# Attention in a hybrid decoder layer: softmax denominators from a column of ones beside each head's value rows

## The chip, the cores and the metric

The kernel runs on one core of a Trainium2 chip. The metric is device time in microseconds for one execution of the whole layer. Five engines work side by side, each through its own instructions in order: TensorE (PE in the profile, its weight loads are PEld), VectorE (DVE), ScalarE (ACT), GpSimd (POOL) and SyncE (SP), which here issues transfers. Matrix products land in PSUM, eight banks of 128 x 512 float32; all else lies in SBUF.

## The reference, cut to what matters

One decoder layer on 512 tokens of width 1024, in float32: a SwiGLU feed-forward half step, a mixer, and a second half step. The mixer's input product gives channels for a gated recurrence (RG-LRU), its gate, and q, k, v for an attention with 8 heads of 64 and 2 key heads. Attention works in blocks of 128 queries against the block before and the block itself, and each head has a sink, a logit without a value:

```
scores = jnp.einsum("bnqkgd,bnjkd->bnkgqj", qb, k_band).astype(jnp.float32) * scale
...
scores = jnp.where(mask[None, :, None, None], scores, MASK_VALUE)
sink = sinks.astype(jnp.float32).reshape(1, 1, N_KV_HEADS, GQA_GROUP, 1, 1)
m = jnp.maximum(jnp.max(scores, axis=-1, keepdims=True), sink)
p = jnp.exp(scores - m)
denom = jnp.sum(p, axis=-1, keepdims=True) + jnp.exp(sink - m)
p = (p / denom).astype(v.dtype)
out = jnp.einsum("bnkgqj,bnjkd->bnqkgd", p, v_band)
...
y = jnp.concatenate([rms_norm(y_lru, g_lru_out), rms_norm(y_attn, g_attn_out)], axis=-1)
return y @ w_o
```

The window is 128, so a query sees exactly 128 keys: those up to itself in its own block, and the later part of the block before.

## The kernel before, in words

Each engine executes its instructions in the order in which the program names them; the order of all engines is written out by hand. Tiles come from pools: tiles with one tag share a fixed number of buffers, and a new tile takes a buffer as it is first written. If all are in use, that first write waits for the last reader of the tile that held the buffer. Three tags matter here. `bank` is the eight PSUM banks. `w` (helper `wt`) has eight buffers of 128 x 512. `t2k` has 38 buffers of 128 x 512 (`NT2K`), shared by the whole layer.

The first feed-forward (up to about 310 us) and the second (from about 530 us) are long series of matrix products. Between them stands the mixer. Weights are split into a rounded part and a remainder (`W.fill` and `W.take`: ScalarE rounds, VectorE subtracts), so that three products of the fast float32 form make one of full precision (`mm3`).

`masks` (line 1319) prepares, on GpSimd, a tile `home` of 128 x 2048: one quarter holds the mask value (`neg`), one the first block of q, one v, and its first 128 columns the first block of k. `in_parts` and the lines around 1510 to 1514 fill it; line 1514 copies v, four blocks of 128 tokens side by side, with both key heads' 64 columns in each.

Attention runs over eight units `(b, n)`: query block b, key head n, four heads each. A loop over `now` from 0 to 9 (line 1717) interleaves the units with other work; at each step the program names

1. `scores(now)`: for n = 0 the score products of the whole block b (four banks for b > 0, two for b = 0), then on VectorE the mask, the row maximum, `nm` (the negative maximum with the sink taken in) and `es` = nm + sink; and at some steps `W.fill`;
2. `pump`: two columns of `mm3` of the recurrence's gate product (`gt`), which fills TensorE's time;
3. `turn_p(now - 1)`: TensorE transposes the unit's four matrices of exponentials, ScalarE copies them to SBUF (`pa`), GpSimd cuts them into the current block's part (`pa`) and the previous block's (`pp`);
4. `exps(now)`: ScalarE, four exponentials of 128 x 128, each with an accumulated row sum (`dsum`), one exponential of `es`; GpSimd adds the two into `den`;
5. `run_due(now - 1)`: steps of the recurrence and of its gate (decay, tanh, scaling by R);
6. one more `pump`, and `values(now - 2)`: the products with v, four heads of 64 columns into half of a bank; both units of a block share the bank `po`. After the second unit VectorE inverts `den` and multiplies, 128 x 512, into `yn` (a `t2k` tile); ScalarE sums its squares later;
7. at now = 5 the four square roots of the recurrence on ScalarE with a table load on each side; at now = 6 their products and two scans on VectorE (`root_u`, `scan`); at now = 8 another scan and a weight split.

After the loop the four `yn` are scaled, transposed (line 1762, `atp`) and, with the recurrence's output, multiplied with `w_o`.

The `t2k` buffers in the middle of the loop: the mixer's input in 16 parts (`xh_mx`, `xl_mx`, read by the gate products until 456 us), `xc`, `r` and `th` with four tiles each, the parts of q for head pairs 0 to 2 (six tiles; those of pair 3 lie in another tag), the parts of k (two), and `up8`, the mask's bytes. `th` is first written at step ci + 1 for channel group ci, `G` at now = 6 and later. The parts of q and k are last read by the score products of block 3, at now = 6, head pair by head pair. In the program as laid out, the second `yn` takes the buffer of pair 0's q.

## Time and profile before

| | us |
|---|---|
| time, median of 3 runs | 845.54 (845.32 to 846.01) |
| span of the profiled execution | 843.6 |
| ScalarE busy, 434.40 to 438.00 and 438.00 to 442.00 | 3.57 of 3.60, 3.97 of 4.00 |
| VectorE busy, 424.00 to 434.40 | 10.02 of 10.40 |
| TensorE busy, 442.00 to 446.00 | 3.65 of 4.00 |
| accumulator reads of the exponentials | 24 and 8, 0.21 each |

The span is that of one profiled execution, from its first instruction to its last; the time of a run holds some 1.9 us more. A row of a timeline gives the start, the duration, the engine, the line of the program, the operation and its tiles; in brackets stands how long the engine had been idle and what released it. Starts lie closer than durations where an engine overlaps the end of one instruction with the start of the next. So the pitch, the distance between two starts, tells what an instruction costs its engine. In the chain of waits a row gives the start, the time that the chain spends there, the engine and the line.

### The profile page before, as it was taken

The page shows a single profiled execution, that of the slowest core. Times are in us where ns is not written, and L with a number is a line of the kernel's source. Part 1 is how long each engine was busy: PE and PEld are TensorE (multiplying, and loading weights), DVE is VectorE, ACT ScalarE, POOL GpSimd, SP SyncE. Part 2 cuts the span into 40 slices and gives each one's busy share as a digit, 9 for nine tenths or more (in the row PEclk, how much of TensorE's full clock was granted, in tenths as well). Part 3 has the DMA queues.
Part 4 walks back from the last instruction along what each step waited for, and adds up shares of the span by engine and source line. Part 5 has one row for each costly group of instructions (what it writes and reads, how often), then busy time and mean ns, then how long its engine had stood idle before and what let it go on. Part 6 is the DMA issues. An engine that isn't in the chain of part 4 may idle for free.

```text
span 843.6 us, 12618 instructions
## 1 busy us (share of the span) xinstructions
PE 834.5 (99%) x4568; PEld 722.6 (86%) x4568; DVE 732.7 (87%) x1020; ACT 523.8 (62%) x874; POOL 201.7 (24%) x214
## 2 busy tenths in 40 slices
PE   9999999999999999999999999999999999999996
PEld 8988888988988998997788899888888888888885
DVE  4978999998979865889899589799998998998996
ACT  6646856666666655456788457436757767666552
POOL 2023000140320333334646055112004113032001
PEclk9999999999999999999999999999999999999999
DMA  7249419397595799222511131169539939769742
GB/s 251 77 131 348 151 59 322 80 254 254 129 248 185 169 261 343 77 79 91 158 50 51 50 110 42 50 137 273 186 108 231 322 91 249 249 154 262 295 137 101
DMA packets 123615, 143.75 MB, mean 170 GB/s; under 512 B 23896, under 2 KB 81568, under 8 KB 123040
## 3 DMA queue, kind: packets, MB, share of 16 engines
q1 hardware_dynamic: 109232, 111.86, 41.6%
q0 software_dynamic: 14176, 30.94, 17.0%
q8 instruction: 36, 0.59, 0.3%
q14 instruction: 27, 0.22, 0.1%
q10 hardware_dynamic: 144, 0.13, 0.0%
HBM read 100.45 MB, written 40.89 MB: 168 GB/s over the span
## 4 chain that ended last, share of the span: by engine, by line
PE 97%; ACT 1%; DVE 1%; DMA 1%; issue 0%; POOL 0%; DVEq 0%; POOLq 0%; ACTq 0%
PE ab L955 10%; PE aa L955 10%; PE da L955 5%; PE db L955 5%; PE yaa L1345 3%; PE bb L955 3%; PE ba L955 3%; PE yda L1345 2%; PE ya L507 2%; PE ya L505 2%; PE ya L506 2%; PE a_first L1205 1%; PE aa L885 1%; PE yab L1875 1%; PE yab L1874 1%; PE yab L1876 1%
## 5 line engine op out<-in xcount | busy, mean ns | idle before, releaser
L1115 POOL DMA_DIRECT2D yp_a<-stage x42 | 36.9, 1085 | 181.2 <-ACT stage L1112 160.9
L1115 POOL DMA_DIRECT2D yp_b<-stage x42 | 36.4, 1091 | 144.6 <-ACT stage L1112 121.1
L505 PE MATMUL ya<-hha,whi_ad 128*128 128x512 f32 x62 | 24.1, 389 | 0.0
L506 PE MATMUL ya<-hla,whi_ad 128*128 128x512 f32 x62 | 24.1, 389 | 0.0
L507 PE MATMUL ya<-hha,wlo_ad 128*128 128x512 f32 x62 | 24.1, 389 | 0.0
L688 POOL TENSOR_TENSOR acca_r<-acca_r,sq_r 128x512 f32<-128x512 f32 x6 | 8.2, 1359 | 51.4 <-ACT sq_r L536 51.4
L1988 POOL TENSOR_TENSOR last<-yp,grow 128x512 f32<-128x512 f32 x3 | 3.9, 1290 | 57.7 <-DVE yp L1983 57.7
L524 PE MATMUL an<-xh_mx,whi_xl 128*128 128x256 f32 x64 | 15.8, 287 | 0.0
L1984 ACT ACTIVATE ysq<-yp 128x512 f32<-128x512 f32 (+1 forms) x9 | 5.3, 585 | 16.5 <-DVE yp L1983 16.0
L525 PE MATMUL an<-xh_mx,wlo_xl 128*128 128x256 f32 x64 | 15.5, 283 | 0.0
L505 PE MATMUL gt<-xh_mx,whi_gt 128*128 128x512 f32 x32 | 14.2, 444 | 0.0
L1112 ACT COPY stage<-yab 128x512 f32<-128x512 f32 x12 | 6.5, 604 | 11.7 <-DMA yp_b<-stage 7.4
L507 PEld LDWEIGHTS ya<-hha,wlo_ad 128*128 128x128 f32 x62 | 11.6, 188 | 2.4
L506 PEld LDWEIGHTS ya<-hla,whi_ad 128*128 128x128 f32 x62 | 11.6, 188 | 2.4
L505 PEld LDWEIGHTS ya<-hha,whi_ad 128*128 128x128 f32 x62 | 11.6, 188 | 2.4
L536 ACT ACTIVATE sq_r<-yp_a 128x256 f32<-128x256 f32 (+1 forms) x10 | 5.0, 502 | 12.9 <-DVE yp_a L678 5.9
L505 PE MATMUL pq<-xh_mx,whi_q 128*128 128x512 f32 x32 | 12.8, 400 | 0.0
L505 PE MATMUL pub<-xh_f,whi_bu 128*128 128x512 f32 x32 | 12.6, 395 | 0.0
L507 PE MATMUL gt<-xh_mx,wlo_gt 128*128 128x512 f32 x32 | 12.6, 394 | 0.0
L505 PE MATMUL pgb<-xh_f,whi_bg 128*128 128x512 f32 x32 | 12.6, 393 | 0.0
L506 PE MATMUL gt<-xl_mx,whi_gt 128*128 128x512 f32 x32 | 12.5, 392 | 0.0
L580 ACT ACTIVATE xh_f<-xT,cols 128x256 fp32r<-128x256 f32 x16 | 8.1, 509 | 7.0 <-DVE xT L719 6.4
(2014 smaller groups left out, 3535.0 us busy)
## 6 DMA issues: line engine op xcount, KB each, us to landing
yp_a<-stage POOLq DMA_DIRECT2D x50, 256.0 KB, 8.9
yp_b<-stage POOLq DMA_DIRECT2D x50, 256.0 KB, 9.2
h_a<-za SPq DMA_DIRECT2D x16, 256.0 KB
hxa<-h_a SPq DMA_DIRECT2D x16, 256.0 KB
h_b<-zb SPq DMA_DIRECT2D x16, 256.0 KB
hxb<-h_b SPq DMA_DIRECT2D x16, 256.0 KB
xn<-in_x SPq DMA_DIRECT2D x8, 256.0 KB
xT_hbm<-xT POOLq DMA_DIRECT2D x2, 1024.0 KB, 9.7
```

Of the source, the lines that this page charges most:

```text
L505: pe.matmul(ps, hi[:, k, :], xh, start=start, stop=False)
L506: pe.matmul(ps, hi[:, k, :], xl, start=False, stop=False)
L507: pe.matmul(ps, lo[:, k, :], xh, start=False, stop=stop)
L524: pe.matmul(ps[:, sl], hi[:, k, :], xh, start=k == 0, stop=False)
L525: pe.matmul(ps[:, sl], lo[:, k, :], xh, start=False, stop=False)
L885: pe.matmul(o, w[:, k, js], x, start=first and i + j + k == 0, stop=k == 3 and i == 2, skip_group_check=True)
L955: pe.matmul(b[tb], x[:, blk], w[:, k, :], start=first and q + k + j == 0, stop=q + k == 2 and j == 2, skip_group_check=True)
L1115: pool.dma_start(o, st.rearrange("p (a b) -> p a b", a=2) if len(o.shape) == 3 else st, accum_op=ALU.add)
L1205: pe.matmul(banks[j][:, HALF[0]], ws[j][part][:, k, :], n1.xs[k][xpart][:, HALF[0]], start=k == 0 and part == xpart, stop=stop and k == KD ...
L1345: pe.matmul(o, a[:, k, ms], x[:, js], start=first and i + k + m % 2 == 0, stop=k == 1 and i == 2, skip_group_check=True)
L1874: pe.matmul(banks[i], hh[:, js], hi[:, k, :], start=first and k == 0, stop=False, skip_group_check=True)
L1875: pe.matmul(banks[i], hh[:, js], lo[:, k, :], start=False, stop=False, skip_group_check=True)
```

## The change

The value rows of each block and key head get a 65th column that holds ones. The product of the exponentials with it is the row sum, so ScalarE's exponentials no longer accumulate, and GpSimd's addition is gone. `home` is laid out anew: k, q, neg, then eight groups of 65 columns. `nm` and `es` become tiles of a whole block; `es` is added and exponentiated once per block, with its second unit. Each unit's values have a bank of their own, and are normalised as soon as the unit is done: VectorE adds the sums' column and `es`, inverts, and multiplies 128 x 256 into its half of `yn`, which so is first written in the block's first unit.

```diff
@@ masks
-        neg = home[0][:, 2 * T:3 * T]
+        neg = home[0][:, P + T:P + 2 * T]
+        pool.memset(home[0][:, P + 2 * T:P + 2 * T + 8 * (HD + 1)].rearrange("p (h d) -> p h d", d=HD + 1)[:, :, HD:], 1.0)
...
-    k0, q0 = home[0][:, :P], home[0][:, T:2 * T]
+    k0, q0 = home[0][:, :P], home[0][:, P:P + T]
...
-            v = home[0][:, 3 * T:]
-            dve.tensor_copy(v, vt)
+            v = home[0][:, P + 2 * T:P + 2 * T + 8 * (HD + 1)]
+            dve.tensor_copy(v.rearrange("p (h d) -> p h d", d=HD + 1)[:, :, :HD], vt.rearrange("p (h d) -> p h d", d=HD))
@@ scores
-        nm = small.tile([P, 4], F32, tag="nm", name=f"nm{b}{n}")
-        dve.scalar_tensor_tensor(nm, mx_, -scale, nsink[:, 4 * n:4 * n + 4], op0=ALU.mult, op1=ALU.min)
-        es = small.tile([P, 4], F32, tag="es", name=f"es{b}{n}")
-        dve.tensor_add(es, nm, sinks[:, 4 * n:4 * n + 4])
-        unit[b, n] = heads, nm, es
+        own = slice(4 * n, 4 * n + 4)
+        if n == 0:
+            unit[b, "nm"] = small.tile([P, 8], F32, tag="nm", name=f"nm{b}")
+        nm = unit[b, "nm"]
+        dve.scalar_tensor_tensor(nm[:, own], mx_, -scale, nsink[:, own], op0=ALU.mult, op1=ALU.min)
+        if n:
+            unit[b, "es"] = small.tile([P, 8], F32, tag="es", name=f"es{b}")
+            dve.tensor_add(unit[b, "es"], nm, sinks)
+        unit[b, n] = heads, nm[:, own]
@@ exps
-            act.activation(sc[:, hs], heads[j], AF.Exp, bias=nm[:, j:j + 1], scale=scale, accum_out=dsum[:, j:j + 1])
-        act.activation(es, es, AF.Exp)
-        if n == 0:
-            unit[b] = small.tile([P, 8], F32, tag="den", name=f"den{b}")
-        pool.tensor_add(unit[b][:, 4 * n:4 * n + 4], dsum, es)
+            act.activation(sc[:, hs], heads[j], AF.Exp, bias=nm[:, j:j + 1], scale=scale)
+        if n:
+            act.activation(unit[b, "es"], unit[b, "es"], AF.Exp)
@@ values
-        if n == 0:
-            unit[b, "o"] = bank(f"po{b}")
-        po = unit[b, "o"]
+        po = bank(f"po{b}{n}")[:, :4 * (HD + 1)]
+        heads = po.rearrange("p (h d) -> p h d", h=4)
+
+        def rows(b):
+            return v[:, (2 * b + n) * (HD + 1):(2 * b + n + 1) * (HD + 1)]
+
         for j in range(4):
             hs = slice(j * P, (j + 1) * P)
-            o = po[:, (4 * n + j) * HD:(4 * n + j + 1) * HD]
+            o = po[:, j * (HD + 1):(j + 1) * (HD + 1)]
             if b > 0:
-                pe.matmul(o, pp[:, hs], v[:, (b - 1) * P + n * HD:(b - 1) * P + (n + 1) * HD], start=True, stop=False)
-            pe.matmul(o, pc[:, hs], v[:, b * P + n * HD:b * P + (n + 1) * HD], start=b == 0, stop=True)
+                pe.matmul(o, pp[:, hs], rows(b - 1), start=True, stop=False)
+            pe.matmul(o, pc[:, hs], rows(b), start=b == 0, stop=True)
+        rden = small.tile([P, 4], F32, tag="rden", name=f"rden{b}{n}")
+        dve.tensor_add(rden.unsqueeze(2), heads[:, :, HD:], unit[b, "es"][:, 4 * n:4 * n + 4].unsqueeze(2))
+        dve.reciprocal(rden, rden)
+        if n == 0:
+            unit[b, "yn"] = t2k(f"yn{b}")
+        yn = unit[b, "yn"]
+        dve.tensor_mul(yn[:, HALF[n]].rearrange("p (h d) -> p h d", h=4), heads[:, :, :HD], rden.unsqueeze(2).to_broadcast([P, 4, HD]))
         if n == 0:
             return
-        rden = small.tile([P, 8], F32, tag="rden", name=f"rden{b}")
-        dve.reciprocal(rden, unit[b])
-        yn = t2k(f"yn{b}")
-        h8 = lambda t: t.rearrange("p (h d) -> p h d", h=8)
-        dve.tensor_mul(h8(yn), h8(po), rden.unsqueeze(2).to_broadcast([P, 8, HD]))
         yns.append(yn)
```

More of the change, by code (lines that the diff above doesn't have):

```diff
@@ L1639, in scores @@
                 heads += [both[:, j, 1, :] for j in range(2)]
-        nm = small.tile([P, 4], F32, tag="nm", name=f"nm{b}{n}")
-        dve.scalar_tensor_tensor(nm, mx_, -scale, nsink[:, 4 * n:4 * n + 4], op0=ALU.mult, op1=ALU.min)
-        es = small.tile([P, 4], F32, tag="es", name=f"es{b}{n}")
-        dve.tensor_add(es, nm, sinks[:, 4 * n:4 * n + 4])
-        unit[b, n] = heads, nm, es
+        own = slice(4 * n, 4 * n + 4)
[7 more added lines that the diff above has]
+        unit[b, n] = heads, nm[:, own]
     def exps(b, n):
-        heads, nm, es = unit[b, n]
-        dsum = small.tile([P, 4], F32, tag="dsum", name=f"dsum{b}{n}")
+        heads, nm = unit[b, n]
         sc = wt(f"sc{b}{n}")
```

## The prediction

> **What bounds the kernel now.** The page comes first: its span, its busy times and, from its fourth part, who carries the chain that ended last.

> ```profile
> span 843.6 us, 12618 instructions
> PE 834.5 (99%) x4568; PEld 722.6 (86%) x4568; DVE 732.7 (87%) x1020; ACT 523.8 (62%) x874; POOL 201.7 (24%) x214
> ...
> PE 97%; ACT 1%; DVE 1%; DMA 1%; issue 0%; POOL 0%; DVEq 0%; POOLq 0%; ACTq 0%
> ```

> TensorE is the bound. A change in attention shows in the time only as a change in TensorE's gaps there. The next view is the chain of waits, read from 422 to 448 us, with the one place in attention where it leaves PE.

> ```profile
> 421.92 0.44 PE pt L1664 x4
> ...
> 434.07 0.24 PE po L1683 x2
> ...
> 434.38 1.51 ACT sc L1652 x8
> ...
> 442.41 0.33 PE pt L1664
> ...
> 443.78 0.24 PE gt L505
> ...
> 446.96 0.52 PE pt L1664 x3
> ...
> 447.84 0.23 PE gt L505
> ```

> TensorE's own timeline, just before those transposes:

> ```profile
> 441.50 0.39 PE L506 MATMUL gt<-xl_mx,whi_gt 128*128 128x512 f32 x1
> 441.73 0.40 PE L507 MATMUL gt<-xh_mx,wlo_gt 128*128 128x512 f32 x1
> ```

> The transposes of unit (3,0) wait for their exponentials one by one. The last gate matmul before them starts at 441.73 and these have a pitch of 0.23, so the transposes could have run from 441.96; four unhindered take 0.44. They end at 443.78: 1.4 us lost. Those of (3,1) take 0.88 instead of 0.44. So 1.8 us is about all that attention can give back.

> Third, the timelines of ScalarE and VectorE around it.

> ```profile
> 423.93 0.37 ACT L1652 ACTIVATE sc<-sc,nm 128x128 f32<-128x128 f32 x1 [0.75 <-DVE nm L1641]
> ...
> 434.38 0.37 ACT L1652 ACTIVATE sc<-sc,nm 128x128 f32<-128x128 f32 x1 [1.59 <-PE po L1683]
> 434.64 0.19 ACT L1652 ACTIVATION_READ_ACCUMULATOR sc<-sc,nm 128x1 f32 x1
> 434.73 0.36 ACT L1652 ACTIVATE sc<-sc,nm 128x128 f32<-128x128 f32 x1
> ...
> 435.76 0.21 ACT L1653 ACTIVATE es<-es 128x4 f32<-128x4 f32 x1
> 435.86 0.64 ACT L1543 ACTIVATE sq_g<-sq_g 128x512 f32<-128x512 f32 x1
> ...
> 445.92 0.40 ACT L1652 ACTIVATE sc<-sc,nm 128x128 f32<-128x128 f32 x1
> ```

> ```profile
> 425.61 0.19 DVE L1688 RECIPROCAL rden<-den 128x8 f32<-128x8 f32 x1
> 425.90 0.69 DVE L1691 TENSOR_TENSOR yn<-po,rden 128x512 f32<-128x512 f32 x1
> 426.50 0.42 DVE L1637 COPY_PREDICATED sc<-up,sc 128x256 f32<-128x256 uint8 x1
> 426.96 0.42 DVE L1638 TENSOR_REDUCE mx<-sc 128x2 f32<-128x256 f32 x1
> 427.30 0.42 DVE L1637 COPY_PREDICATED sc<-up,sc 128x256 f32<-128x256 uint8 x1
> ...
> 430.67 1.12 DVE L1540 SCALAR_TENSOR_TENSOR sq_g<-sq_g,gt 128x512 f32<-128x512 f32 x1
> 431.71 0.42 DVE L1637 COPY_PREDICATED sc<-up,sc 128x256 f32<-128x256 uint8 x1
> ...
> 433.42 0.16 DVE L1641 SCALAR_TENSOR_TENSOR nm<-mx,nsink 128x4 f32<-128x4 f32 x1
> ...
> 438.29 0.69 DVE L1426 TENSOR_TENSOR gt<-gt,R_mx 128x512 f32<-128x512 f32 x1
> 439.51 1.29 DVE L1587 TENSOR_TENSOR xc<-xc,th 128x512 f32<-128x512 f32 x2 [0.53 <-ACT th L1584]
> ...
> 444.67 0.94 DVE L1641 SCALAR_TENSOR_TENSOR nm<-mx,nsink 128x4 f32<-128x4 f32 x1
> ```

> VectorE runs its instructions in the order of the program with hardly an idle stretch here. So what the change puts into its queue, and what that must wait for, counts most.

> **The change part by part.** *ScalarE.* The 32 reads of the accumulator go. One exponential with its read has a pitch of 0.35 (434.38 to 434.73); its read starts 0.26 after it. Nothing shows an exponential without a read: its pitch lies between 0.35 (no gain) and 0.26, and I take 0.26, since only the read stands between. That is 0.09 each, 0.35 in a unit, 2.9 in all. Four of the eight activations of es go too, 0.10 each (435.76 to 435.86). Only what shortens the two TensorE gaps is worth time: unit (2,1) delivers 0.35 earlier, and the last transpose of (3,0) comes 3 x 0.09 earlier still, 0.6; and 0.35 in the gap of (3,1). Together −1.0, if nothing else moves.

> [...]

> *GpSimd* loses eight den additions of 0.2 and gets one more memset near 300 us. The mask it delays a little is ready about 304 and read by VectorE at 317.0 (rows below), so this is hidden; without that cover it would cost at most the 2.08 of the full memset beside it.

> ```profile
> 302.34 1.36 POOL L1325 TENSOR_SCALAR_AFFINE_SELECT upf<-home 128x512 f32<-128x512 f32 x1
> ...
> L1327 DVE CAST up<-upf x1: 420/420/420, 317.0 to 317.0; 128x512 uint8<-128x512 f32 x1
> ```

> *TensorE.* The 112 value matmuls move 65 columns instead of 64. Eight of 64 columns take 0.84, 0.105 each; four transposes of 128 columns 0.44, 0.11 each. Twice the columns at the same price: one column more costs 0, at most 1/64 of 112 x 0.11, 0.2. I take 0. The copy of v into strides moves as many elements as before.

> ```profile
> 419.64 0.84 PE po L1684 x8
> ```

> *VectorE.* In a block before: es twice, reciprocal 0.29 and multiply 0.60 (425.61, 425.90, 426.50). After: es once, and per unit an addition, a reciprocal and a half multiply. A small dependent step is 0.29 (that reciprocal), down to 0.2; a half multiply is 0.35, by the reduce of 256 columns from PSUM (426.96 to 427.30). That is 0.85 for each unit. A second unit's share stays as it was (0.85 for 0.89); a first unit's is new: 0.85 less 0.2 for its es.

> These new steps are instructions that wait for the value matmuls, one place earlier in the queue than any did. In block 0 nothing holds them: VectorE is behind, and only its 0.65 delays the row maximum of (1,1), for which ScalarE waits already (0.75 at 423.93). The exponentials shift 0.5, and with them a bank for the second half of the scores of block 2: TensorE +0.4.

> In block 1 they meet something larger: storage. yn comes from 38 buffers of 2 KB, and by the code these are alive then: 16 parts of the mixer's input (the gate matmuls read them to 456), xc, r and th, four each, six parts of q, two of k, up8, and yn of block 0: 38. The first to come free are the q parts of head pair 0, when the scores of block 3 have read them. Before, the second yn takes just that buffer: its multiply comes after the last value matmul of block 1, and TensorE goes on to those scores at once.

> ```profile
> L1621 PE MATMUL sc<-kTl,qT0h x6: 275/279/279, 415.4 to 434.7; 64*128 64x256 f32 x6
> ...
> 435.26 0.35 PE L1621 MATMUL sc<-kTh,qT2h 64*128 64x256 f32 x2
> ...
> 440.29 0.39 PE L1684 MATMUL po<-home,pa 128*128 128x64 f32 x2
> ```

> In the change this multiply stands in `values(1, 0)`, ahead of the scores of (2,1), which ran at 431.71. VectorE reaches it near 432.3 and must wait for 434.7 + 0.28 + 0.4 (TensorE's shift), 435.35. Behind it are queued the masks and maxima of (2,1): they start at 435.35 + 0.35 = 435.7 and nm is ready 1.87 later (431.71 to 433.58 before), 437.6. ScalarE's exponentials of (2,1), begun at 434.38, move by 3.2, wherever their own buffer wait lands. TensorE feels it twice. First, of eight banks, two hold gates, one or two hold values and two hold the scores of (2,1): block 3's last score bank must wait for two exponentials, 437.6 + 0.26 + 0.37 = 438.2, where TensorE wrote it at about 435.3: it idles some 2.5 us. Second, the tail of unit (2,1) on ScalarE (tables, roots, exponentials of (3,0)) arrives 3.2 − 0.35 later; the last of those exponentials ends at 441.89 + 2.85 + 3 x 0.26 + 0.37 = 445.9, and the transposes end at 446.0 instead of 443.78: +2.2.

> Then the new steps of `values(2, 0)` stand ahead of the square roots' products and the scans. They wait for matmuls of which the last pair started at 440.29, so ended near 440.5, and that end 2.9 later at 443.4; +0.85, and the work that started at 439.51 starts at 444.3. The row maximum of (3,1), ready at 445.6, had lost 0.8 to a slow nm; without that I put it at 449.7. The exponentials of (3,1) move from 445.92 to 449.7, the transposes end 0.78 + 0.37 + 0.17 later at 451.0 instead of 447.84: +3.2. `values(3, 0)` likewise holds back a scan and a weight split, so the last yn comes 4.0 late. Before, ScalarE's scaling of the second yn ended at 455.9, 0.5 ahead of the transpose that reads it (rows below); with yn 4.0 late and TensorE 3.2, that slack is overdrawn by 0.3.

> ```profile
> 454.56 1.33 ACT L1708 ACTIVATE yn<-yn,rat 128x512 f32<-128x512 f32 x2
> ...
> 456.28 1.75 PE atp L1762 x16
> ```

> *The sum.* +3.5, the −0.35s of ScalarE included: 843.6 + 3.5 = 847.1 of span. The runs' median is 845.54, 1.9 above this execution's span; so 849.0. After 458 us the chain before is TensorE alone up to the tail, with one VectorE wait of 0.7, so a delay stays.

> **The rivals.**

> *In-order waits only (846.5).* If a buffer is free for the second yn, the VectorE waits at `values(2, 0)` and `values(3, 0)` remain. The first holds the roots' products from 439.51 to 441.6, moves the exponentials of (3,1) to about 447.1, TensorE +0.6; the second makes the last yn 1.5 late, +0.4 at the transposes of yn: +1.0. For it: nothing in the rows shows a wait for storage outright. Against it: the count of 38.

> *Only ScalarE's gain (844.5).* The other side, faster. If the new steps find their matmuls done and their buffers free, −1.0 remains. It decides at `values(2, 0)`: VectorE would have to reach it after 440.5. Before, its neighbour ended at 438.98, which speaks against it. [...]

> *The accumulator was free anyway.* If an exponential keeps its pitch of 0.35, the change doesn't lighten ScalarE: the sum loses its 0.6 of gains, 849.6.

> *Banks run out as well (851.5).* If the first score banks of block 3 are also given out late, TensorE waits for `values(1, 1)` on VectorE, which stands behind the scores of (2,1) (2.0) and a step of 0.7: about 2.5 more than the forecast. For it: the eight banks are all in use there. Against it: the two banks of (2,0)'s scores are free by then.

> **How the numbers follow.** Forecast 0.45, accumulator free anyway 0.08, banks as well 0.17, in-order waits only 0.2, ScalarE's gain alone 0.1. The forecast's own range, with 0.06 or 0.09 for an exponential, 0 to 0.2 for the columns, and 0.2 or 0.29 for each small step, is 847.4 to 850.6. For 8 in 10 I go from 845.6, below the in-order case, to 852.0, above the banks. 0.2%, about what a measurement of this kernel can tell from no change, is 1.7 us: slower means above 847.2, faster below 843.9. The first three cases are slower, 0.70, less 0.02 for the forecast's low tail: 0.68. The in-order case, that 0.02 and 0.04 of ScalarE's gain make 0.26 for the same; its other 0.06, which needs nearly all the 1.8 us of gaps, is faster.

> **What would show it.** No accumulator reads, and exponentials 0.26 apart. VectorE idle 2 to 3 us before the multiply of block 1's first unit, near 432, and TensorE idle about 2.5 us within the scores of block 3. An idle VectorE ahead of the same steps of blocks 2 and 3. The transposes of yn about 3.5 us later; from there on the two traces should keep that distance. If VectorE doesn't idle at 432, the count of buffers was wrong; if TensorE has no new gap, the order was not the bound.

## The result, and the profile after

| kernel | median, us | range of the runs | ratio to before, 95% interval |
|---|---|---|---|
| before | 845.56 | 845.32 to 846.01 | |
| changed | 858.14 | 854.91 to 858.63 | 1.014, 1.0126 to 1.0155 |

The change makes the kernel 1.4% slower: 12.6 us, where the forecast had 3.5. The profiled execution took 858.63 us, with a span of 856.9. Its page, with the span, the busy times, the clock that TensorE was granted in 40 slices, and the shares of the chain that ended last:

```profile
span 856.9 us, 12591 instructions
...
PE 842.5 (98%) x4568; PEld 730.0 (85%) x4568; DVE 734.0 (86%) x1032; ACT 520.8 (61%) x838; POOL 199.2 (23%) x207
...
PEclk9999999999999999999986999999999999999999
...
PE 96%; DVE 2%; DMA 1%; issue 0%; ACT 0%; SPq 0%; DVEq 0%; ACTq 0%
```

TensorE is busy for 8.0 us more with the same 4568 matmuls, and two slices of the clock row, 8 and 6, are no longer full. So more than half of the loss looks like time in which TensorE works at a lower clock; a run below tests it. The rest is idle time, as its waits show (the waiting line, what it waits for, total, times, longest):

```profile
PE pt L1666 <- ACT sc L1656: 3.7, 1, 3.7
PE sc L1622 <- ACT sc L1656: 2.1, 1, 2.1
```

Both on TensorE's timeline, with two gate matmuls 11 us behind the second:

```profile
437.86 0.58 PE L1622 MATMUL sc<-kTh,qT2h 64*128 64x256 f32 x1 [2.12 <-ACT sc L1656]
...
454.69 1.25 PE L1666 MATMUL pt<-ident,sc 128*128 128x128 f32 x4 [3.70 <-ACT sc L1656]
...
465.98 0.63 PE L507 MATMUL gt<-xh_mx,wlo_gt 128*128 128x512 f32 x1
466.41 0.63 PE L505 MATMUL gt<-xh_mx,whi_gt 128*128 128x512 f32 x1
```

The first is the score bank of block 3, the second the transposes of unit (3,1). What is late lies on VectorE, whose timeline has:

```profile
431.64 0.18 DVE L1692 RECIPROCAL rden<-rden 128x4 f32<-128x4 f32 x1
434.87 0.42 DVE L1696 TENSOR_TENSOR yn<-po,rden 128x256 f32<-128x256 f32 x1 [3.05 <-PE sc L1622]
...
445.98 0.16 DVE L1691 TENSOR_TENSOR rden<-po,es 128x4 f32<-128x4 f32 x1 [2.04 <-PE po L1689]
```

The first multiply of block 1 waits 3.05 us for a matmul of the *scores*, line 1622, which it does not read: a wait for the buffer of q. The first step of unit (2,0) waits 2.04 us for its value products. On ScalarE's timeline the exponentials of (2,1) and (3,1) stand behind these:

```profile
437.18 1.14 ACT L1656 ACTIVATE sc<-sc,nm 128x128 f32<-128x128 f32 x4 [4.58 <-DVE nm L1645]
...
454.27 1.14 ACT L1656 ACTIVATE sc<-sc,nm 128x128 f32<-128x128 f32 x4 [5.78 <-DVE nm L1645]
```

And TensorE's clock by stretches of 2 us. PE's busy time comes first after the length, the clock third from the end; 1.00 is the full clock, 0.50 half:

```profile
434.00:436.00 2.00, 1.69 (x17) 1.22 (x16) 1.09 (x3) 0.00 (x0) 0.00 (x1) 1.00 0.00 0
436.00:438.00 2.00, 0.14 (x2) 0.14 (x2) 1.86 (x8) 0.82 (x4) 0.00 (x0) 0.73 0.00 0
438.00:440.00 2.00, 2.00 (x12) 1.71 (x13) 1.90 (x6) 1.98 (x5) 0.00 (x0) 0.50 0.00 0
440.00:442.00 2.00, 2.00 (x6) 1.54 (x5) 0.98 (x3) 1.99 (x5) 0.00 (x0) 0.50 0.00 0
442.00:444.00 2.00, 2.00 (x8) 1.70 (x7) 0.69 (x1) 1.97 (x4) 0.00 (x0) 0.57 0.00 0
444.00:446.00 2.00, 2.00 (x18) 1.95 (x18) 0.02 (x1) 2.00 (x7) 1.44 (x3) 1.00 0.00 0
...
454.00:456.00 2.00, 1.30 (x5) 1.08 (x6) 1.88 (x7) 1.25 (x6) 0.00 (x0) 0.50 0.00 0
...
466.00:468.00 2.00, 2.00 (x7) 1.59 (x6) 1.34 (x6) 1.76 (x5) 0.07 (x1) 0.59 1.09 387
```

Behind each gap the clock is 0.50, though TensorE is busy again. The matmuls show it too: the gate matmuls, 0.23 apart in the prediction's rows, are 0.43 apart here (465.98 to 466.41). From the starts of work after the two gaps to the ends of half clock (0.57 in the stretch from 442 and 0.59 in that from 466 put them at about 443.7 and 467.6) are 5.9 and 12.9 us. If half of that is lost, it is 2.9 + 6.5 = 9.4 us, beside 5.8 of idle time. The transposes of yn start 13.6 us later than before (456.28), and from there to the end the distance hardly changes (the spans differ by 13.3):

```profile
469.88 1.75 PE atp L1769 x16
```

### The profile page after: what moved, and what is told of

Its sections match the earlier page's. It is cut to its first block, busy times and chain, and to the rows that moved or that the text cites. A ratio compares the mean times of both kernels' runs of the same rounds, so it can differ in the third digit from the quotient of the medians.

```text
span 856.9 us, 12591 instructions
## 1 busy us (share of the span) xinstructions
PE 842.5 (98%) x4568; PEld 730.0 (85%) x4568; DVE 734.0 (86%) x1032; ACT 520.8 (61%) x838; POOL 199.2 (23%) x207
## 4 chain that ended last, share of the span: by engine, by line
PE 96%; DVE 2%; DMA 1%; issue 0%; ACT 0%; SPq 0%; DVEq 0%; ACTq 0%
PE ab L955 10%; PE aa L955 10%; PE da L955 5%; PE db L955 5%; PE yaa L1346 3%; PE bb L955 3%; PE ba L955 3%; PE yda L1346 2%; PE ya L507 2%; PE ya L506 2%; PE ya L505 2%; PE aa L885 1%; PE a_first L1205 1%; PE yab L1881 1%; PE yab L1883 1%; PE yab L1882 1%
## 5 line engine op out<-in xcount | busy, mean ns | idle before, releaser
L505 PE MATMUL ya<-hha,whi_ad 128*128 128x512 f32 x62 | 24.1, 389 | 0.0
L506 PE MATMUL ya<-hla,whi_ad 128*128 128x512 f32 x62 | 24.1, 389 | 0.0
L507 PE MATMUL ya<-hha,wlo_ad 128*128 128x512 f32 x62 | 24.1, 389 | 0.0
L505 PE MATMUL gt<-xh_mx,whi_gt 128*128 128x512 f32 x32 | 16.1, 504 | 0.0
L506 PE MATMUL gt<-xl_mx,whi_gt 128*128 128x512 f32 x32 | 14.1, 440 | 0.0
L507 PE MATMUL gt<-xh_mx,wlo_gt 128*128 128x512 f32 x32 | 14.0, 436 | 0.0
L1656 ACT ACTIVATE sc<-sc,nm 128x128 f32<-128x128 f32 x24 | 6.9, 371 | 11.5 <-DVE nm L1645 11.5
L507 PEld LDWEIGHTS ya<-hha,wlo_ad 128*128 128x128 f32 x62 | 11.6, 188 | 2.4
L506 PEld LDWEIGHTS ya<-hla,whi_ad 128*128 128x128 f32 x62 | 11.6, 188 | 2.4
L505 PEld LDWEIGHTS ya<-hha,whi_ad 128*128 128x128 f32 x62 | 11.6, 188 | 2.4
L1689 PE MATMUL po<-home,pa 128*128 128x65 f32 x64 | 13.2, 309 | 0.0
L536 ACT ACTIVATE sq_r<-yp_a 128x256 f32<-128x256 f32 (+1 forms) x10 | 5.0, 502 | 12.9 <-DVE yp_a L678 5.9
L505 PE MATMUL pq<-xh_mx,whi_q 128*128 128x512 f32 x32 | 12.8, 399 | 0.0
L505 PE MATMUL pub<-xh_f,whi_bu 128*128 128x512 f32 x32 | 12.6, 395 | 0.0
```

Source lines behind the costliest of these rows:

```text
L505: pe.matmul(ps, hi[:, k, :], xh, start=start, stop=False)
L506: pe.matmul(ps, hi[:, k, :], xl, start=False, stop=False)
L507: pe.matmul(ps, lo[:, k, :], xh, start=False, stop=stop)
L1689: pe.matmul(o, pc[:, hs], rows(b), start=b == 0, stop=True)
```

## The experiments

Two theories. *Storage and clock*: the wait for q's buffer makes the first gap, the second follows from it, and both cost the clock. *In-order waits*: VectorE's new steps ahead of the root products and scans make the second gap by themselves. The runs in short:

| kernel | median, us | mean granted clock of the runs |
|---|---|---|
| changed | 858.14 | 0.986 to 0.992 |
| mask in spare columns (storage undone) | 852.23 | 0.990 to 0.997 |
| divisions moved back (order undone) | 848.06 | 0.995 to 0.998 |
| both undone | 844.61 | 0.997 to 0.999 |
| divided at the block's end | 844.27 | 0.997 to 0.999 |
| changed, TensorE kept busy in the gaps | 850.62 | 0.998 |
| mask in spare columns, TensorE kept busy | 847.54 | 0.998 to 0.999 |

**The mask in spare columns.** One buffer more for yn.

```diff
-    up8 = t2k("up8", U8).rearrange("p (a b) -> p a b", a=NB)
-    up8f = up8.rearrange("p a b -> p (a b)")
...
+        up8f = home[0][:, 1792:1792 + P].bitcast(U8)
```

> The changed kernel, but the mask of block 0 to 3 lies in unused columns of the tile that holds the ones, so that one 2 KB buffer is free for block 1's result. Storage and clock theory (VectorE's 3.05 us wait for q's buffer makes TensorE idle 2.1 us, the granted clock then falls to half for 6 us, the second gap of 3.7 us follows from the first, and a second stretch of half clock from that): VectorE's wait is gone, no gap of TensorE over 1 us in attention, granted clock 0.99 throughout, 844.5 to 847 us. In-order theory (VectorE's new steps ahead of the root products and the scans make the second gap, storage only the first): the gap of 2.1 us is gone, one of 2 to 4 us ahead of the transposes of (3,1) stays, with half clock behind it, 852 to 856 us.

Measured: 852.23 us (848.36 to 853.35), ratio 1.0073 (1.0053 to 1.0094). VectorE's timeline no longer has the wait at 432, but keeps the other one:

```profile
431.87 0.42 DVE L1696 TENSOR_TENSOR yn<-po,rden 128x256 f32<-128x256 f32 x1
...
440.34 0.16 DVE L1691 TENSOR_TENSOR rden<-po,es 128x4 f32<-128x4 f32 x1 [1.72 <-PE po L1689]
```

TensorE's waits have one line left:

```profile
PE pt L1666 <- ACT sc L1656: 2.8, 1, 2.8
```

The storage wait makes the first gap. The second does not follow from it: without it there are still 2.8 us, and half clock behind them. The first theory falls in that point.

```profile
450.00:454.00 4.00, 4.00 (x18) 3.71 (x17) 0.83 (x2) 1.64 (x3) 1.27 (x2) 0.50 0.00 0
```

**Divided at the block's end.** The accumulators, the ones and the sinks' terms stay; only the early division goes.

```diff
+        unit[b, n] = heads
+        if n:
+            norm(b, 0)
+            norm(b, 1)
+
+    def norm(b, n):
+        heads = unit[b, n]
```

> The changed kernel, but both units of a block are divided at the block's end, as before the change; the two accumulators, the columns of ones and the denominators' terms stay. Storage and clock theory and in-order theory alike: both causes are gone, so 844.5 to 846.5 us, and no gap over 1 us in attention. If the loss came from the second accumulator bank or from the 65-column products, it stays or grows (two banks are held longer here): 850 us or more.

Measured: 844.27 us, ratio 0.9987 (0.9979 to 0.9996); its profile has no TensorE wait over 0.3 us in attention. So the loss does not come from the second accumulator or the 65 columns: all of it is the early division. Without that the rest of the change wins 1.1 us (845.40 for the kernel before in the same series). This version is faster than both kernels.

**No sums in the kernel before.**

```diff
-            act.activation(sc[:, hs], heads[j], AF.Exp, bias=nm[:, j:j + 1], scale=scale, accum_out=dsum[:, j:j + 1])
+            act.activation(sc[:, hs], heads[j], AF.Exp, bias=nm[:, j:j + 1], scale=scale)
...
-        pool.tensor_add(unit[b][:, 4 * n:4 * n + 4], dsum, es)
+        pool.tensor_copy(unit[b][:, 4 * n:4 * n + 4], es)
```

> The kernel before, but ScalarE does not accumulate the exponentials and nothing takes the sums' place (the denominators hold the sinks' terms alone). If the exponentials are on the path that sets the end, as the prediction costed them: exponentials 0.26 us apart and 844.5 us (0.6 to 1.0 less than before). If ScalarE's work is hidden behind TensorE: 845.3 to 845.7 us.

This kernel leaves out the row sums, so it does not compute the layer; it serves for its time alone. Measured: 843.81 us, ratio 0.9981 (0.9972 to 0.9990), 1.6 us less than before. **The accumulator on again**, in the kernel that divides at the block's end, is the test from the other side:

```diff
-            act.activation(sc[:, hs], heads[j], AF.Exp, bias=nm[:, j:j + 1], scale=scale)
+            act.activation(sc[:, hs], heads[j], AF.Exp, bias=nm[:, j:j + 1], scale=scale, accum_out=dsum[:, j:j + 1])
```

> The kernel that divides at the block's end, with the exponentials accumulating again (the sums are written and not used). If what it wins against the kernel before is ScalarE's 0.09 us for each exponential: exponentials 0.35 us apart and 845.0 to 845.8 us. If the gain came from elsewhere (GpSimd's sums taken out, fewer sinks' terms): 844.0 to 844.6 us.

Measured: 845.79 us, 1.5 more than with the accumulator off. ScalarE's timeline of this kernel has the pitch of 0.35 again:

```profile
434.96 0.36 ACT L1657 ACTIVATE sc<-sc,nm 128x128 f32<-128x128 f32 x1
435.21 0.20 ACT L1657 ACTIVATION_READ_ACCUMULATOR sc<-sc,nm 128x1 f32 x1
435.31 0.37 ACT L1657 ACTIVATE sc<-sc,nm 128x128 f32<-128x128 f32 x1
```

The reads of the accumulator were on the path that sets the end. They are worth 1.5 to 1.6 us, more than the gain of 1.1: what else the change does costs some 0.5. Without accumulation the times are 844.27 with the rest of the change and 843.81 without it, with accumulation 845.79 and 845.34; the second difference is at the edge of the noise (ratio 1.0006, 0.9996 to 1.0015).

**TensorE kept busy in the gaps.** Products that are overwritten fill both gaps; the waits themselves stay.

```diff
+            if b == 3 and j == 2:
+                for _ in range(9):
+                    pe.matmul(score_banks[b, 0][1], kh[:, :P], kh, start=True, stop=True)
...
+        if (b, n) == (3, 1):
+            kh = kT[0]
+            for _ in range(16):
+                pe.matmul(pt, kh[:, :P], kh, start=True, stop=True)
```

> The changed kernel with TensorE kept busy where it idled: 9 products of 128x512 (about 0.23 us each) into the score bank that is free ahead of the second half of block 3's scores, and 16 into the bank of the transposes of (3,1); both are overwritten. Clock theory: the granted clock stays at 0.99, the two waits stay as time, and the time is 858.1 less the two stretches at half clock (3 and 6.4 us), 847 to 851 us. If instead the chain of VectorE's waits sets the end and half clock only fills it, 856 to 859 us.

Measured: 850.62 us (850.28 to 852.08). TensorE's timeline has both fillings, and the clock's windows are at 1.00 throughout:

```profile
434.86 2.33 PE L1620 MATMUL sc<-kTh 128*128 128x512 f32 x9
...
448.39 3.81 PE L1670 MATMUL pt<-kTh 128*128 128x512 f32 x16
452.04 0.60 PE L1673 MATMUL pt<-ident,sc 128*128 128x128 f32 x4
```

The same waits at full clock cost 7.5 us less. That is the price of the clock, and the estimate of 9.4 was 1.9 too high. Of these, 0.3 are a wait for the last yn that TensorE now arrives early enough to have. Some 0.7 stand ahead of and in the transposes of (3,0): at full clock these again follow their exponentials one by one, and from the gate product ahead of them to the one behind them it is 443.85 to 445.11, in the changed kernel 446.99 to 447.57. The rest stays open. The profiled execution is the slowest of the four (852.08); TensorE idles 1.7 us between 480 and 700 us there, 0.3 in the changed kernel's profile, so most of that excess seems to lie behind attention.

**The divisions of (2,0) and (3,0) moved back** behind the root products and scans, and likewise behind the last scan and the weight split; the storage is as in the changed kernel.

```diff
-            values(*units[now - 2])
+            values(*units[now - 2], now in (6, 8))
...
             for ci in (2, 3):
                 scan(ci)
+            norm(*units[4])
```

> The changed kernel, but VectorE divides units (2,0) and (3,0) after the root products and scans instead of ahead of them; the mask stays in its 2 KB buffer, so the wait for q's buffer stays. If the two waits add (storage makes the first gap, the order the second): the gap of 2.1 us within block 3's scores stays with half clock behind it, the gap ahead of the transposes of (3,1) shrinks from 3.7 to under 2 us, and the time is 848 to 853 us. If the first wait alone causes both gaps: 857 to 859 us, as in the changed kernel.

Measured: 848.06 us (847.78 to 849.57), ratio 1.0037 (1.0023 to 1.0051). Its TensorE waits:

```profile
PE sc L1622 <- ACT sc L1656: 2.1, 1, 2.1
PE pt L1666 <- ACT sc L1656: 0.4, 1, 0.4
```

As expected in time and in both gaps, but not in the clock. The same 2.1 us as in the changed kernel have no half clock behind them, by its windows:

```profile
436.00:438.00 2.00, 0.00 (x0) 0.00 (x0) 1.90 (x7) 0.66 (x3) 0.00 (x0) 1.00 0.00 0
438.00:440.00 2.00, 1.98 (x16) 1.67 (x17) 1.86 (x8) 1.98 (x5) 0.00 (x0) 1.00 0.00 0
```

One of its four executions has a mean clock of 0.995, so there a part of the clock was lost as well.

**Both undone**, this edit and the mask's together:

> The mask in the unused columns and the units (2,0) and (3,0) divided after the root products and scans: both undone, the rest of the change as it is, with units (0,0) and (1,0) divided early. Theory of two waits: no gap over 1 us, clock 0.99 or more, 843.8 to 845 us, as with the division at the block's end (844.27). If a third cause is left, 846 us or more.

Measured: 844.61 us, ratio 0.9995 (0.9986 to 1.0004). No third cause is left. That the units (0,0) and (1,0) are still divided early brings nothing over the block's end (844.27).

**GpSimd's work moved away from VectorE's.** With the order as in the change, VectorE's root products and scans themselves took longer. In the kernel with TensorE kept busy:

```profile
443.59 1.72 DVE L1588 TENSOR_TENSOR xc<-xc,th 128x512 f32<-128x512 f32 x2
445.23 3.79 DVE L1593 TENSOR_TENSOR_SCAN xc<-r,xc 128x512 f32<-128x512 f32 x2
```

and in the one with the divisions moved back:

```profile
442.12 1.29 DVE L1588 TENSOR_TENSOR xc<-xc,th 128x512 f32<-128x512 f32 x2 [0.33 <-ACT th L1585]
443.33 2.33 DVE L1593 TENSOR_TENSOR_SCAN xc<-r,xc 128x512 f32<-128x512 f32 x2
```

In the first, GpSimd works beside them from 444.00 on, nearly without a pause:

```profile
444.00 0.76 POOL L1679 TENSOR_SCALAR_AFFINE_SELECT pp<-pa 128x512 f32<-128x512 f32 x1 [10.49 <-ACT pa L1675]
444.83 0.97 POOL L1680 TENSOR_SCALAR_AFFINE_SELECT pa<-pa 128x512 f32<-128x512 f32 x1
445.77 4.33 POOL L1588 TENSOR_TENSOR xc<-xc,th 128x512 f32<-128x512 f32 x2
```

in the second it starts only at 444.66, when the second scan is under way. The run takes GpSimd's two root products away from there, in the kernel with the mask in spare columns:

```diff
+        if now == 7:
+            for ci in (0, 1):
+                root_u(ci)
         if now == 6:
-            for ci in range(KC):
+            for ci in (2, 3):
                 root_u(ci)
```

> The kernel with the mask in the unused columns, but GpSimd's two root products come a step later, behind the masks of (3,0). If GpSimd's work beside VectorE's is what makes VectorE's two root products (1.72 us instead of 1.29) and two scans (3.79 instead of 2.33) slow: these fall to 1.3 and 2.4 to 2.9 us, the gap of 2.8 us ahead of the transposes of (3,1) shrinks by 1 to 1.8 us, and the time falls from 852.2 to 845.5 to 850 us. If they are slow for another reason, they and the time stay (850 to 853 us).

Measured: 851.87 us (848.57 to 852.33): the time is a miss. On VectorE's timeline the scans fall by a microsecond, and the slowness moves on to the next small step:

```profile
441.23 1.72 DVE L1588 TENSOR_TENSOR xc<-xc,th 128x512 f32<-128x512 f32 x2
442.87 2.76 DVE L1593 TENSOR_TENSOR_SCAN xc<-r,xc 128x512 f32<-128x512 f32 x2
...
447.24 0.77 DVE L1645 SCALAR_TENSOR_TENSOR nm<-mx,nsink 128x4 f32<-128x4 f32 x1
```

That step ends at 448.0, and so does the first of GpSimd's moved products (446.74 and half of 2.49):

```profile
446.74 2.49 POOL L1588 TENSOR_TENSOR xc<-xc,th 128x512 f32<-128x512 f32 x2
```

The gap shrinks from 2.8 to 2.3 us only, and in three of four executions the clock is still lost (0.990). In the fourth, the profiled one (848.57, mean clock 0.997), half clock lasts only from 448.5 to 451.9:

```profile
448.00:450.00 2.00, 1.47 (x5) 1.16 (x6) 1.93 (x5) 1.53 (x6) 1.22 (x1) 0.63 0.00 0
450.00:452.00 2.00, 2.00 (x10) 1.80 (x8) 1.15 (x3) 1.57 (x3) 1.28 (x2) 0.52 0.00 0
```

At that mean clock the kernel without this edit took 848.36. That GpSimd slows VectorE's work is shown, by the scans; that moving it helps the time is not.

**The mask in spare columns, TensorE kept busy**, with such products ahead of the transposes of (3,1):

```diff
+            for _ in range(12):
+                pe.matmul(pt, kh[:, :P], kh, start=True, stop=True)
```

> The kernel with the mask in the unused columns (852.2 us, one gap of 2.8 us ahead of the transposes of (3,1)), with 12 products of 128x512 into the bank of these transposes ahead of them, which the transposes overwrite. Clock theory: the wait stays as time and half clock goes, so 844.4 + 2.8, 847 to 848.2 us, with the granted clock at 0.997 or more. If the time above 844.4 is not the clock's: 851 to 853 us. The prediction's rival of in-order waits had 846.5 us for this without a term for the clock.

Measured: 847.54 us (846.96 to 847.80). So of the 7.6 us that the order alone costs (852.23 to 844.61), 4.7 are the clock's and 2.9 the wait's.

**One gap of chosen length.** In the kernel that divides at the block's end, two, four or seven copies hold ScalarE, so that TensorE idles once, ahead of the transposes of (3,1).

```diff
+        for _ in range(2 if (b, n) == (3, 1) else 0):
+            act.copy(sc, v[:, :T])
```

> The kernel that divides at the block's end (844.27 us), with two needless copies of 128x512 on ScalarE ahead of the exponentials of (3,1), so that TensorE idles once, for about 1 us, ahead of the transposes of (3,1). If only a longer gap costs the clock: granted clock 0.99 or more, 845 to 845.6 us. If any gap does: over 847 us.

> The same with four copies: one gap of about 2.1 us. If a gap of this length costs the clock, as the first of the changed kernel's did (2.1 us, then 6 us at half clock, so 3 us more): 848 to 851 us. If half clock came of something else there: 846 to 847 us.

> The same with seven copies: one gap of about 3.6 us. If it costs as the second of the changed kernel's (3.7 us, then 13 us at half clock, 6.4 us more): 852 to 855 us. If half clock lasts as after the shorter gap: 849 to 851.5 us.

| copies | gap in the trace, us | median, us | range | mean clock |
|---|---|---|---|---|
| 2 | 0.4 | 844.87 | 844.34 to 845.42 | 0.997 to 0.999 |
| 4 | 1.7 | 847.00 | 845.54 to 851.60 | 0.997 to 0.999, 0.990 to 0.992 in three of ten |
| 7 | 3.3 | 853.63 | 852.75 to 853.91 | 0.990 |

The gaps came out 0.3 to 0.6 us shorter than meant. A gap of 0.4 costs 0.6. With four copies the cost is 1.3 to 3.2 us in seven executions of ten and 6.4 to 7.3 in three, which neither of the two expected cases covers; the gap of 1.7 is that of the traced execution, which kept its clock. A gap of 3.3 costs 8.5 to 9.6, nearly three times its length. The windows of that kernel, from the last of the idle time on, show how long the half clock lasts:

```profile
448.00:449.00 1.00, 0.03 (x1) 0.04 (x1) 1.00 (x2) 0.97 (x3) 0.00 (x0) 0.61 0.00 0
449.00:460.00 11.00, 11.00 (x44) 10.10 (x45) 2.73 (x8) 4.82 (x12) 3.73 (x4) 0.50 0.28 95
460.00:461.00 1.00, 1.00 (x4) 0.81 (x3) 0.94 (x3) 0.51 (x1) 0.00 (x0) 0.50 0.00 0
461.00:462.00 1.00, 1.00 (x4) 0.75 (x4) 0.40 (x2) 0.97 (x4) 0.00 (x0) 0.57 0.00 0
```

## Why the prediction was right about the waits and wrong about the time

*Right: the wait for storage.* VectorE stops at block 1's first multiply, 3.05 us by the trace, from 431.8 to 434.87 where 432.3 to 435.35 was forecast; the first edit takes the wait away by one buffer. The row maximum nm of (2,1) is ready at 437.1 (437.6 forecast), and the gap within block 3's scores is 2.1 us (2.5 forecast). Alone, this wait costs 848.06 − 844.61 = 3.5 us.

*Right: ScalarE's gain.* The exponentials are 0.26 apart ((1.14 − 0.37) / 3), the value that the prediction took. It made that 1.0 us; the two runs on the accumulator show 1.6 and 1.5, so here too the size was low. The 0.06 for an exponential that stands beside 0.09 in the forecast's range is shown by no run: by the rows of the runs without and with accumulation it is 0.35 − 0.26 = 0.09.

*Right: the 65 columns cost nothing.* From the first start of a unit's 16 value products to the gate product behind them it is 1.71 us before (428.32 to 430.03) and 1.70 in the changed kernel (428.20 to 429.90). *Not quite right: that nothing else costs.* The version divided at the block's end is some 0.5 us slower than the gain of the reads alone would have it; which part of the change that is, GpSimd's memset included, was not tried apart.

*Wrong, the step that failed: the sum has no term for TensorE's clock.* It added the delays of VectorE and ScalarE to a TensorE that runs its matmuls at one pitch, 0.23 for a gate matmul, whether it has idled or not. Its two gaps, 2.5 us within the scores and one ahead of the transposes of (3,1), were there to be asked about. The runs put in its place: 858.14 − 850.62 = 7.5 us of lower clock, more than the two gaps themselves (5.8). Of the 9.1 us by which the forecast of 849.0 was short, this is 7.5.

*Too small: the second delay.* The prediction had the root products start at 444.3 and the row maximum of (3,1) at 449.7, so 5.4 us for the products, the scans, the masks and the maxima. With the clock kept, they start at 443.59, even earlier, and the maximum is ready at 450.8: 7.2 us, since products and scans together took 5.51 (1.72 + 3.79) instead of 3.62 (1.29 + 2.33). Delayed, they fall into GpSimd's masks of (3,0) and its own root products. With full clock the time is 850.62 against the forecast of 849.0; the 1.6 us between them is about this term, 1.9.

*The rivals.* In-order waits alone: 846.5 was forecast; the run with the mask moved has 852.2, and 847.5 with the clock kept, so that mechanism was real, undersized by 1.0, and without a clock again. The rival stood beside the forecast as an alternative; both happened. Only ScalarE's gain (844.5): what the kernels divided at the block's end (844.27) and with both undone (844.61) reach, not this one. With two banks for a block's halves, early division of two blocks of four (844.61) is no faster than late division of all (844.27). An accumulator that was free: refuted by 1.5 us. Banks run out as well: no such wait, since TensorE's waits have only the two lines shown.

## What to carry to other kernels

A new instruction in the queue of an in-order engine brings two waits with it, for its data (here 2.04 us for the value products of (2,0)) and for the buffer that it writes (3.05 us for that of q); count the living buffers at the new place, and look at what stands behind it. Where TensorE sets the end, price a gap not by its length alone. Here a gap of 0.4 us cost 0.6, and one of 3.3 cost 8.5 to 9.6, with half clock behind it; with four copies, 1.7 us in the trace, three executions of ten lost the clock. So ask what the matmuls behind a gap cost at half clock, and compare with filling the gap or moving the work that makes it. When work slides in time, look up what runs beside it at the new place, on GpSimd too, before its old duration is used: here two scans went from 2.33 to 3.79 us.

## What the runs showed of the hardware

```profile
436.00:437.00 1.00, 0.00 (x0) 0.00 (x0) 0.93 (x4) 0.00 (x0) 0.00 (x0) 0.95 0.00 0
...
443.00:444.00 1.00, 1.00 (x4) 0.86 (x4) 0.69 (x1) 0.99 (x3) 0.00 (x0) 0.63 0.00 0
...
453.00:454.00 1.00, 0.00 (x0) 0.00 (x0) 0.95 (x3) 0.00 (x0) 0.00 (x0) 0.99 0.00 0
...
467.00:468.00 1.00, 1.00 (x5) 0.79 (x4) 0.67 (x3) 1.00 (x3) 0.00 (x0) 0.69 1.08 386
```

By these the clock falls at 436.9, returns at 443.7, falls at 454.0 and returns at 467.6. The distances are 6.8, 10.2 and 13.6 us, about two, three and four times the 3.4 that half clock lasted in the run with GpSimd's products moved (448.5 to 451.9); whether that is more than chance is not shown. And the clock fell inside the gaps, the first time 1.2 us after TensorE had gone idle (435.7), the second time 3.0 after (451.0). How long TensorE must be idle for it is not settled.

*The half clock lasts longer than the gap.* In the changed kernel TensorE had its clock back 5.9 us after the end of the gap in the first case and 12.9 in the second, and with seven copies about 12.9 behind the gap of 3.3 us (448.97 to 461.86, by 0.57 in the window from 461), while it was busy all the time (2.00 of 2.00 us in each stretch from 438 to 444 and from 456 to 468; with seven copies 11.00 of 11.00 from 449 to 460). Counted from the fall, half clock lasts 3.4 us once (GpSimd's products moved), 6.8 once, and 13.6 or 13.7 three times (the second gap; the seven copies, 448.2 to 461.9; the mask in spare columns, 449.2 to 462.9); what sets the length is not shown. In the changed kernel's long case half of that time (6.5 of 13.6 us) went to value products of 65 columns (457.02 to 460.29 and 461.72 to 464.99), and the clock came back 2.6 us after the last run of gate matmuls of 512 columns had begun (464.99); with the mask in spare columns it was 3.8 (459.10). Whether the small products are what holds it down was not tried.

*VectorE's work can slow beside GpSimd's.* Two scans took 3.79 us instead of 2.33, two products 1.72 instead of 1.29, and a step on four columns 0.77 instead of 0.16. For the scans the run with GpSimd's products moved shows it (2.76, without GpSimd's products beside them); for the other two it is only seen that GpSimd worked beside them. The ends fall together, though whether it is a wait or slower work was not tried: the step of 0.77 ends at 448.0 and GpSimd's product beside it too, and before the change the same step, 0.94 long in the prediction's rows, ends at 445.6, again with a GpSimd product (444.31 and half of 2.52).
